# Where the weight splits, token sums and modulation sums of a trunk's first mixer run

## The chip, the cores and the metric

The kernel runs on one core of one Trainium2 chip. The metric is the device time of one execution in microseconds (us). A core has a matrix engine (PE, whose weight loads are shown as PEld), a vector engine (DVE), an activation engine (ACT), a general engine (POOL) and an engine that here only issues transfers (SP). Each takes its instructions in order; semaphores tie them together.

## The reference

Two layers of a trunk over 512 tokens of width 1024, all in float32. Every half layer is a sandwich with a modulation that comes from one vector c:

```python
def sandwich(x, mod, g_pre, g_post, fn):
    shift, scale, gate = mod
    h = rms_norm(x, g_pre) * (1.0 + scale[:, None]) + shift[:, None]
    return x + gate[:, None] * rms_norm(fn(h), g_post)
```

`mod` is `silu(c) @ w + b`, split in three. The first `fn` is the mixer that the change touches. It projects h to u, q, f, v and g. u goes through a pool mixer: for four groups of 128 features, a mean over the last 2, 4, 8 or 16 tokens less u, times a small matrix and a scale. q, f, v and g go through HGRN with 4 heads: with f' = lb + (1 - lb) sigmoid(f) as decay and k = (1 - lb) sigmoid(-f) as key, o[t] = q[t] applied to the decayed sum of k[s] v[s] over s <= t; then an RMS norm, a gain and silu(g). Both results are concatenated and projected (w_ho). The other three `fn` are a SwiGLU, a dilated attention and a SwiGLU.

## The kernel before, in words

**Layout.** h lies with features on the 128 partitions, 8 tiles of 512 tokens (k = 0 to 7). Every float32 product is made of three matmuls: an operand is split into a rounded part `hi` and the rest `lo = x - hi`, and hi*hi, lo*hi and hi*lo are added in a PSUM bank. A weight block is 128x1024 (512 KB). `load_next` (transfer L326, on SP) brings the next block, `split_next` makes `hi` by ACT (L351) and `lo` by `sub` (L284). `sub` puts every `by`-th subtraction on POOL, all on DVE when `by` is 0; for weights `by` is `share[0]`, which is 1 from the start (all on POOL), 2 from the gate on and 3 behind the mixer.

**Modulation.** 96 rows of the modulation's matrix, each 128x1025, are loaded into three buffers (`ada_load`, L390) and multiplied with silu(c) and summed by one DVE operation (`ada_half`, L403). Two halves are a step (`ada_step`): 0 to 7 give shift and scale of the first sandwich's eight tiles, 8 to 11 its gate, 12 to 19 shift and scale of the second. A small operation (L412, for all eight of a later sandwich L417) makes `s1 = (1 + scale) * gain`. The load of half i takes the buffer of half i - 3. `ADA` caps the steps in three stages of the mixer: 12 while the values are made, 20 in the pool stage, 20 in the gate's.

**First projections (to L550).** x is squared by ACT (L487) and added by DVE; PE sums over the partitions, DVE and POOL (a power, L475) make 1/rms, and PE spreads it over a bank (`rb_bank`). Then the loop over k, with the order of PE, ACT, DVE and SP written by hand (`hold` to `release`): DVE has `xr = x * rows` (L512, L538); ACT makes h_hi from it (L522, scale and shift as operands); DVE makes h again (`t`, L536) and h_lo = t - h_hi (L539). Block k of w_qf is split one round ahead, two halves of modulation for k + 1 are made, and 24 matmuls (L263) go into eight banks: q and f of four heads.

**The mixer (L880 to L1180).** Here a planner in the build orders the instructions of each engine by its own costs. ACT makes silu(q) and two sigmoids of f (L905, L906), DVE scales them (L908, L909). Twelve `level`s (128 small matmuls, L929, taken out by DVE, L930) and twelve `grow`s (DVE, L940, L941, L943) make the heads' products inside a 64-token tile; between them PE makes the values (w_v, 96 matmuls). The pool stage takes w_u block by block: ACT copies u (L1041), POOL makes the token sums by doubling (L1047, ten operations of 128x512), DVE finishes (L1053 to L1056), a split and three matmuls follow. Then come the cross blocks (L1081, L1091), copied by DVE (L1084, L1092), the gate (w_g, 96 matmuls) and the four heads (L1126 to L1164), among whose matmuls the first part of w_ho's lies.

**Later stages** are not touched: the second half of w_ho, SwiGLU, attention and SwiGLU, whose orders are written by hand with fixed places for splits (`ENDS`).

Of the kernel before, what the change touches and what calls it, by code (L numbers as in the profile page):

```python
# [12 lines left out]
F32 = mybir.dt.float32  # L13
# [7 lines left out]
ND = D // P  # L21
# [33 lines left out]
LAST_WARM = 3, 5  # L55
ADA = 12, 20, 20
G_SHARE = 2
EARLY = 3
# [122 lines left out]
def trunk(ctx: ExitStack, tc: tile.TileContext, a: dict, out: bass.AP, last: int = 3):  # L181
# [95 lines left out]
    turn = [0]  # L277
    share = [1]

# [115 lines left out]
    def ada_half(k):  # L395
        s, j = divmod(ada["at"], 12)
        i = 2 * ada["at"] + k
        if i < ada["next"]:
            return
        ada_load(i)  # L400
        w = ada["loaded"].pop(i)
        ada["next"] = i + 1
        dve.scalar_tensor_tensor(w, w, 1.0, sil, ALU.mult, ALU.mult, accum_out=mods[:, s, 2 * j + k : 2 * j + k + 1])  # L403

    def ada_step(until):
        if ada["at"] >= min(until, 48):
            return
        s, j = divmod(ada["at"], 12)
        for k in range(2):
            ada_half(k)  # L410
        if j < 8 and s == 0:
            dve.scalar_tensor_tensor(  # L412
                s1[:, s, j : j + 1], mods[:, s, 2 * j : 2 * j + 1], 1.0, npre[:, s, j : j + 1], ALU.add, ALU.mult
            )
        elif j == 7:
# [52 lines left out]
    tr.free(c_r)  # L468

    def rstd(sums, n, cols):  # L470

        v = col(cols)
        dve.tensor_scalar(v, sums, 1.0 / n, EPS, ALU.mult, ALU.add)  # L473
        r = col(cols)
        pool.tensor_tensor(r, v, mhalf[:, 0:cols], ALU.pow)  # L475
        return r
# [23 lines left out]
    tr.free(acc)  # L500
    ada_half(0)
    r = rstd(bk[b][:, 0:4], D, 4)
    ada_step(1)
    bk.free(b)
    weights(w_qf)
    keep_warm(WARM[1])
    rb_bank = bk.get()
    spread(rb_bank, r, 4)
    rb_r = tr.get(1)
    xr_rs = [tr.get(1) for _ in range(2)]  # L510
    xr = [tr.ap(z) for z in xr_rs]
    dve.tensor_tensor(xr[0], xT[:, 0, :], bk[rb_bank], ALU.mult)  # L512
    keep_warm(WARM[2])
# [4 lines left out]
    for k in range(ND):  # L518
        ada_load(2 * k + 2)
        ada_step(k + 1)  # L520
        ada_load(2 * k + 3)
        act.activation(h_hi[:, k, :], xr[k % 2], AF.Identity, bias=shift(0, k), scale=s1[:, 0, k : k + 1])  # L522
        if k == 0:
            act.activation(tr.ap(rb_r), bk[rb_bank], AF.Copy)
            bk.free(rb_bank)
            banks8.append(bk.get())
        hi, lo = weights(w_qf + k)
        for _ in range(1 + k % 2):
            load_next()
        if state["split"] <= w_qf + k + 1 < w_v:  # L530
            split_next()
        if k == 6:
            sp.dma_start(ar.ap(masks_r), a["masks"])
        t_r = tr.get(1)
        t = tr.ap(t_r)
        dve.tensor_scalar(t, xr[k % 2], s1[:, 0, k : k + 1], shift(0, k), ALU.mult, ALU.add)  # L536
        if k + 1 < ND:
            dve.tensor_tensor(xr[(k + 1) % 2], xT[:, k + 1, :], tr.ap(rb_r), ALU.mult)  # L538
        dve.tensor_tensor(h_lo[:, k, :], t, h_hi[:, k, :].bitcast(F32), ALU.subtract)  # L539
        tr.free(t_r)  # L540
        passes = ((hi, h_hi), (lo, h_hi), (hi, h_lo))
# [4 lines left out]
        weights_done(w_qf + k)  # L546
    for z in (rb_r, *xr_rs):
        tr.free(z)
# [353 lines left out]
    for h in range(4):  # L902
# [134 lines left out]
    for g in range(4):  # L1037
# [38 lines left out]
    for pr in range(2):  # L1076
# [5 lines left out]
        for i in range(2):  # L1082
            ps = slice(64 * i, 64 * i + 32)
            dve.tensor_copy(A[pr][ps, :, 64 * i + 32 : 64 * i + 64], bk[b][ps, 0:256].rearrange("p (n t) -> p n t", n=8))  # L1084
        bk.free(b)
        grow(pr, 32)
    for pr in range(2):
        b = bk.get()
        for n in range(8):
            o = n * P  # L1090
            pe.matmul(bk[b][0:64, n * 64 : n * 64 + 64], KS[pr][:, o : o + 64], QP[pr][:, o + 64 : o + 128], start=True, stop=True, skip_group_check=True)  # L1091
        dve.tensor_copy(A[pr][0:64, :, 64:128], bk[b][0:64, :].rearrange("p (n t) -> p n t", n=8))  # L1092
        bk.free(b)
# [9 lines left out]
    ahead.update(load=9, split=4, f=4)  # L1103
    share[0] = G_SHARE
    for h in range(4):
# [476 lines left out]
```

## Time and profile before

| | us |
|---|---|
| median of 3 runs | 1296.45 (1294.95 to 1298.38) |
| the profiled execution, in all | 1293.51 |
| its span, first to last instruction | 1291.70 |
| loop over k, first to last matmul | 17.63 to 72.34 |
| values to gate | 72.34 to 185.17 |
| heads and the first part of w_ho | 185.17 to 217.41 |

A line of the timeline gives start, duration, engine, line of the source, operation, output <- inputs, shape and count, and in brackets how long the engine had been idle and which work ended that. The granted clock (PEclk) is the share of full speed that PE was given; 0.985 over the execution. Grouped lines give the count, the busy time and the mean of one in ns.

### The profile page before, as it was taken

The page shows a single profiled execution, that of the slowest core. Times are in us where ns is not written, and L with a number is a line of the kernel's source. Part 1 is how long each engine was busy: PE and PEld are TensorE (multiplying, and loading weights), DVE is VectorE, ACT ScalarE, POOL GpSimd, SP SyncE. Part 2 cuts the span into 40 slices and gives each one's busy share as a digit, 9 for nine tenths or more (in the row PEclk, how much of TensorE's full clock was granted, in tenths as well). Part 3 has the DMA queues.
Part 4 walks back from the last instruction along what each step waited for, and adds up shares of the span by engine and source line. Part 5 has one row for each costly group of instructions (what it writes and reads, how often), then busy time and mean ns, then how long its engine had stood idle before and what let it go on. Part 6 is the DMA issues. An engine that isn't in the chain of part 4 may idle for free.

```text
span 1291.7 us, 20674 instructions
## 1 busy us (share of the span) xinstructions
PE 1236.8 (96%) x8672; PEld 1093.5 (85%) x8672; DVE 646.6 (50%) x965; ACT 453.5 (35%) x743; POOL 271.3 (21%) x141
## 2 busy tenths in 40 slices
PE   7897798999999999999999999999899999999997
PEld 5675588998888889999989978778898888889997
DVE  7997975766444222345767324336864111213415
ACT  4241434543222222224544324335742222222313
POOL 4641531312111102131311111011411111121002
PEclk9998899999999999999999999999999999999999
DMA  8855344144554223242348412124416222223301
GB/s 289 309 165 193 114 164 147 38 143 179 196 196 147 82 82 98 98 147 66 115 129 289 170 59 71 36 98 148 144 63 235 82 82 82 65 93 95 108 1 66
DMA packets 50383, 164.25 MB, mean 127 GB/s; under 512 B 5809, under 2 KB 11081, under 8 KB 50290
## 3 DMA queue, kind: packets, MB, share of 16 engines
q1 hardware_dynamic: 50290, 162.93, 37.2%
q8 instruction: 68, 1.11, 0.4%
q14 instruction: 25, 0.20, 0.0%
HBM read 160.78 MB, written 2.13 MB: 126 GB/s over the span
## 4 chain that ended last, share of the span: by engine, by line
PE 81%; DVE 12%; ACT 3%; issue 2%; POOL 1%; DMA 1%; SPq 0%; DVEq 0%; ACTq 0%; POOLq 0%
PE bank L263 78%; DVE ada_w L403 4%; PE bank L1374 1%; DVE t L642 1%; PE bank L1343 1%; DVE swing L941 1%; DVE swing L284 1%; DVE f L646 1%; DVE swing L940 1%; POOL cst L475 1%; DVE h L681 0%; DVE t L603 0%; DVE r L284 0%; POOL h L284 0%; DMA f<-x 0%
## 5 line engine op out<-in xcount | busy, mean ns | idle before, releaser
L263 PE MATMUL bank<-h,r 128*128 128x512 f32 (+1 forms) x2104 | 467.8, 364 | 15.5 <-DVE f L930 8.0
L263 PEld LDWEIGHTS bank<-h,r 128*128 128x128 f32 x2104 | 364.9, 192 | 78.5 <-ACT h L522 9.0
L263 PE MATMUL bank<-h,swing 128*128 128x512 f32 (+1 forms) x1664 | 325.1, 343 | 3.6 <-ACT swing L351 2.2
L263 PEld LDWEIGHTS bank<-h,swing 128*128 128x128 f32 x1664 | 268.5, 191 | 39.9 <-ACT swing L351 2.4
L284 POOL TENSOR_TENSOR r<-f,r 128x1024 fp32r<-128x1024 f32 x39 | 100.2, 2570 | 391.1 <-PE bank L263 289.0
L351 ACT ACTIVATE r<-f 128x1024 fp32r<-128x1024 f32 x104 | 109.1, 1057 | 134.5 <-PE bank L263 105.5
L263 PE MATMUL bank<-o,swing 128*128 128x256 f32 x1280 | 153.7, 276 | 0.0
L403 DVE SCALAR_TENSOR_TENSOR ada_w<-ada_w,sil 128x1025 f32<-128x1025 f32 x96 | 143.7, 1513 | 11.8 <-DMA ada_w<-ada 11.7
L263 PEld LDWEIGHTS bank<-o,swing 128*128 128x128 f32 x1280 | 149.1, 188 | 0.1
L284 DVE TENSOR_TENSOR r<-f,r 128x1024 fp32r<-128x1024 f32 (+1 forms) x51 | 65.1, 1277 | 167.3 <-PE bank L263 110.5
L284 POOL TENSOR_TENSOR swing<-f,swing 128x1024 fp32r<-128x1024 f32 x27 | 66.5, 2462 | 255.7 <-PE bank L263 209.0
L284 DVE TENSOR_TENSOR swing<-f,swing 128x1024 fp32r<-128x1024 f32 x45 | 59.9, 1335 | 119.9 <-PE bank L263 80.9
L351 ACT ACTIVATE swing<-f 128x1024 fp32r<-128x1024 f32 x80 | 83.5, 1058 | 85.9 <-PE bank L263 42.2
L263 PE MATMUL bank<-o,r 128*128 128x256 f32 x832 | 101.7, 275 | 0.0
L263 PEld LDWEIGHTS bank<-o,r 128*128 128x128 f32 x832 | 97.8, 188 | 0.1
L1196 ACT ACTIVATE t<-bank 128x512 f32<-128x512 f32 (+1 forms) x52 | 27.2, 531 | 175.3 <-PE bank L263 175.3
L263 PE MATMUL bank<-h,o 128*128 128x512 f32 (+1 forms) x312 | 80.8, 345 | 2.5 <-DVE h L681 1.7
L263 PE MATMUL bank<-r,h 128*128 128x512 f32 x288 | 71.9, 397 | 0.0
L263 PEld LDWEIGHTS bank<-r,h 128*128 128x128 f32 x288 | 61.7, 249 | 6.3 <-issue 0.4
L263 PEld LDWEIGHTS bank<-h,o 128*128 128x128 f32 x312 | 55.0, 188 | 11.1 <-DVE h L681 2.1
L475 POOL TENSOR_TENSOR cst<-cst 128x2 f32<-128x2 f32 (+1 forms) x19 | 17.9, 940 | 210.2 <-DVE cst L473 210.2
L284 DVE TENSOR_TENSOR o<-f,o 128x256 fp32r<-128x256 f32 (+2 forms) x37 | 24.8, 687 | 74.1 <-ACT o L565 70.3
(187 smaller groups left out, 1046.9 us busy)
## 6 DMA issues: line engine op xcount, KB each, us to landing
ada_w<-ada SPq DMA_DIRECT2D x96, 512.5 KB, 4.9
f<-w_fi SPq DMA_DIRECT2D x88, 512.0 KB, 4.8
f<-w_fo SPq DMA_DIRECT2D x44, 512.0 KB, 3.5
f<-w_aqk SPq DMA_DIRECT2D x24, 512.0 KB, 3.8
f<-w_av SPq DMA_DIRECT2D x12, 512.0 KB, 4.4
f<-w_qf SPq DMA_DIRECT2D x8, 512.0 KB, 4.7
f<-w_ho SPq DMA_DIRECT2D x8, 512.0 KB, 3.5
f<-x SPq DMA_DIRECT2D x8, 256.0 KB, 3.1
```

What stands on the lines that cost most here:

```text
L263: i = pe.matmul(o, lhsT, rhs, start=start, stop=stop, skip_group_check=True)
L284: eng.tensor_tensor(o, x, y, ALU.subtract)
L351: act.activation(hi, w, AF.Copy)
L403: dve.scalar_tensor_tensor(w, w, 1.0, sil, ALU.mult, ALU.mult, accum_out=mods[:, s, 2 * j + k : 2 * j + k + 1])
L475: pool.tensor_tensor(r, v, mhalf[:, 0:cols], ALU.pow)
L642: dve.tensor_tensor(us[i], us[i], rows, ALU.mult)
L646: (pool if i < 2 else dve).tensor_tensor(x, x, us[i], ALU.add)
L940: dve.tensor_tensor(qv, qv, t_first.unsqueeze(2).broadcast_to([P, n, L]), ALU.mult)
L941: dve.tensor_tensor(kv, kv, t_second.unsqueeze(2).broadcast_to([P, n, L]), ALU.mult)
L1196: act.activation(tr.ap(sa)[:, cols], a, AF.Silu)
L1343: pe.matmul(o, qc, kc, start=True, stop=True, skip_group_check=True)
L1374: pe.transpose(bk[b][:, seg * P : (seg + 1) * P], sc[:, i * P : (i + 1) * P], ident)
```

## The change

- All weight splits of the mixer's weights go to DVE: `share[0]` is 0 until the end of the mixer.
- h takes two DVE operations per tile: `u = x * s1 * rows`, then ACT makes h_hi = u + shift, and DVE h_lo = (u + shift) - h_hi.
- At the start two more transfers are issued ahead (modulation half 2, weight block 1). The second half of step 0 waits for POOL's power, and `s1` of a tile is made by `scale_of` as soon as its scale is there. In the loop the two halves stand on either side of h_lo; block 0 is split in the loop and no longer before it.
- The scalings of f' and k (L908, L909) and the copies of the cross blocks (L1084, L1092) go from DVE to ACT.
- The token sums (L1047) go from POOL to DVE.
- `ADA` is 9, 12, 16: one step with the values, three in the pool stage, four with the gate, and the last four with the heads, where `ada_step(20)` stood already.

```diff
-ADA = 12, 20, 20
-G_SHARE = 2
+ADA = 9, 12, 16
-    share = [1]
+    share = [0]
+    def scale_of(k):
+        dve.scalar_tensor_tensor(s1[:, 0, k : k + 1], mods[:, 0, 2 * k : 2 * k + 1], 1.0, npre[:, 0, k : k + 1], ALU.add, ALU.mult)
...
     load_next()
+    ada_load(2)
+    load_next()
...
     ada_half(0)
+    ada_load(3)
+    scale_of(0)
     r = rstd(bk[b][:, 0:4], D, 4)
-    ada_step(1)
+    tc.add_manual_dep(ada_half(1).ins, newest_rstd[0], SYNC, reason="they would slow each other down")
+    ada_load(4)
     bk.free(b)
-    weights(w_qf)
...
-    dve.tensor_tensor(xr[0], xT[:, 0, :], bk[rb_bank], ALU.mult)
...
     for k in range(ND):
-        ada_load(2 * k + 2)
-        ada_step(k + 1)
-        ada_load(2 * k + 3)
-        act.activation(h_hi[:, k, :], xr[k % 2], AF.Identity, bias=shift(0, k), scale=s1[:, 0, k : k + 1])
+        u = tr.ap(us_rs[k % 2])
+        rows = tr.ap(rb_r) if k else bk[rb_bank]
+        dve.scalar_tensor_tensor(u, xT[:, k, :], s1[:, 0, k : k + 1], rows, ALU.mult, ALU.mult)
+        hi, lo = weights(w_qf + k)
+        act.activation(h_hi[:, k, :], u, AF.Identity, bias=shift(0, k))
...
-        hi, lo = weights(w_qf + k)
+        ada["at"] = k + 1
+        if k + 1 < ND:
+            ada_half(0)
+            ada_load(2 * k + 5)
         for _ in range(1 + k % 2):
             load_next()
-        if state["split"] <= w_qf + k + 1 < w_v:
+        dve.scalar_tensor_tensor(h_lo[:, k, :], u, shift(0, k), h_hi[:, k, :].bitcast(F32), ALU.add, ALU.subtract)
+        if k + 1 < ND:
+            ada_half(1)
+            ada_load(2 * k + 6)
+            scale_of(k + 1)
             split_next()
...
-        dve.tensor_scalar(t, xr[k % 2], s1[:, 0, k : k + 1], shift(0, k), ALU.mult, ALU.add)
-        if k + 1 < ND:
-            dve.tensor_tensor(xr[(k + 1) % 2], xT[:, k + 1, :], tr.ap(rb_r), ALU.mult)
-        dve.tensor_tensor(h_lo[:, k, :], t, h_hi[:, k, :].bitcast(F32), ALU.subtract)
...
-        dve.tensor_scalar(FT[h // 2][:, sl], FT[h // 2][:, sl], lb1[:, h : h + 1], lb[:, h : h + 1], ALU.mult, ALU.add)
-        dve.tensor_scalar(KS[h // 2][:, sl], KS[h // 2][:, sl], lb1[:, h : h + 1], None, ALU.mult)
+        act.activation(FT[h // 2][:, sl], FT[h // 2][:, sl], AF.Identity, bias=lb[:, h : h + 1], scale=lb1[:, h : h + 1])
+        act.activation(KS[h // 2][:, sl], KS[h // 2][:, sl], AF.Copy, scale=lb1[:, h : h + 1])
...
-            pool.tensor_tensor(nxt[:, PADW:], cur[:, PADW:], cur[:, PADW - n : U_w - n], ALU.add)
+            dve.tensor_tensor(nxt[:, PADW:], cur[:, PADW:], cur[:, PADW - n : U_w - n], ALU.add)
...
-            dve.tensor_copy(A[pr][ps, :, 64 * i + 32 : 64 * i + 64], ...)
+            act.activation(A[pr][ps, :, 64 * i + 32 : 64 * i + 64], ..., AF.Copy)
...
-        dve.tensor_copy(A[pr][0:64, :, 64:128], ...)
+        act.activation(A[pr][0:64, :, 64:128], ..., AF.Copy)
...
-    share[0] = G_SHARE
```

More of the change, by code (lines that the diff above doesn't have):

```diff
@@ L258, in release @@
         held[0].__exit__(None, None, None)
+    SYNC = mybir.DependencyInfo(mybir.DependencyClass.Sync, mybir.DependencyReason.DATA)
     NOSYNC = mybir.DependencyInfo(mybir.DependencyClass.NoSync, mybir.DependencyReason.DATA)
@@ L402, in ada_half @@
         ada["next"] = i + 1
-        dve.scalar_tensor_tensor(w, w, 1.0, sil, ALU.mult, ALU.mult, accum_out=mods[:, s, 2 * j + k : 2 * j + k + 1])
+        return dve.scalar_tensor_tensor(w, w, 1.0, sil, ALU.mult, ALU.mult, accum_out=mods[:, s, 2 * j + k : 2 * j + k + 1])
     def ada_step(until):
@@ L410, in ada_step @@
             ada_half(k)
[L411 to L415, printed above, removed]
+        if j == 7:
             sc = mods[:, s, 0:16].rearrange("p (k two) -> p k two", two=2)[:, :, 0]
@@ L468, in trunk @@
     tr.free(c_r)
+    newest_rstd = [None]
     def rstd(sums, n, cols):
@@ L474, in rstd @@
         r = col(cols)
-        pool.tensor_tensor(r, v, mhalf[:, 0:cols], ALU.pow)
+        newest_rstd[0] = pool.tensor_tensor(r, v, mhalf[:, 0:cols], ALU.pow).ins.name
         return r
@@ L509, in trunk @@
     rb_r = tr.get(1)
-    xr_rs = [tr.get(1) for _ in range(2)]
-    xr = [tr.ap(z) for z in xr_rs]
-    dve.tensor_tensor(xr[0], xT[:, 0, :], bk[rb_bank], ALU.mult)
+    us_rs = [tr.get(1) for _ in range(2)]
     keep_warm(WARM[2])
@@ L533, in trunk @@
             sp.dma_start(ar.ap(masks_r), a["masks"])
-        t_r = tr.get(1)
-        t = tr.ap(t_r)
-        dve.tensor_scalar(t, xr[k % 2], s1[:, 0, k : k + 1], shift(0, k), ALU.mult, ALU.add)
-        if k + 1 < ND:
-            dve.tensor_tensor(xr[(k + 1) % 2], xT[:, k + 1, :], tr.ap(rb_r), ALU.mult)
-        dve.tensor_tensor(h_lo[:, k, :], t, h_hi[:, k, :].bitcast(F32), ALU.subtract)
-        tr.free(t_r)
         passes = ((hi, h_hi), (lo, h_hi), (hi, h_lo))
@@ L546, in trunk @@
         weights_done(w_qf + k)
-    for z in (rb_r, *xr_rs):
+    for z in (rb_r, *us_rs):
         tr.free(z)
@@ L1083, in trunk @@
             ps = slice(64 * i, 64 * i + 32)
-            dve.tensor_copy(A[pr][ps, :, 64 * i + 32 : 64 * i + 64], bk[b][ps, 0:256].rearrange("p (n t) -> p n t", n=8))
+            act.activation(A[pr][ps, :, 64 * i + 32 : 64 * i + 64], bk[b][ps, 0:256].rearrange("p (n t) -> p n t", n=8), AF.Copy)
         bk.free(b)
@@ L1091, in trunk @@
             pe.matmul(bk[b][0:64, n * 64 : n * 64 + 64], KS[pr][:, o : o + 64], QP[pr][:, o + 64 : o + 128], start=True, stop=True, skip_group_check=True)
-        dve.tensor_copy(A[pr][0:64, :, 64:128], bk[b][0:64, :].rearrange("p (n t) -> p n t", n=8))
+        act.activation(A[pr][0:64, :, 64:128], bk[b][0:64, :].rearrange("p (n t) -> p n t", n=8), AF.Copy)
         bk.free(b)
```

## The prediction

> **What bounds the kernel now.** I read the page's head first: it says which engine fills the span.
>
> ```profile
> span 1291.7 us, 20674 instructions
> PE 1236.8 (96%) x8672; PEld 1093.5 (85%) x8672; DVE 646.6 (50%) x965; ACT 453.5 (35%) x743; POOL 271.3 (21%) x141
> ```
>
> PE is busy for 96%, so only time in which PE waits, or runs at a lower granted clock, can be won. The change touches nothing behind the mixer; I cut what lies before that into stages by the windows view (us, then busy us of PE, PEld, DVE, ACT, POOL, then PEclk, DMA share, GB/s).
>
> ```profile
> 17.63:72.34 54.71, 47.80 (x193) 36.60 (x194) 53.89 (x67) 21.13 (x26) 29.93 (x10) 0.97 0.79 275
> 72.34:99.99 27.65, 27.65 (x473) 21.57 (x476) 26.01 (x42) 11.58 (x19) 10.69 (x5) 1.00 0.56 191
> 185.17:217.41 32.24, 27.45 (x216) 26.47 (x214) 18.12 (x30) 11.98 (x37) 6.52 (x5) 0.95 0.31 98
> 72.34:185.17 112.83, 97.62 (x1211) 76.11 (x1211) 98.27 (x149) 38.82 (x68) 42.72 (x23) 0.89 0.49 165
> ```
>
> The first row is the loop over the eight first weight blocks, the second the values' stage, the third the four heads, and the last the whole middle (values, levels, token sums, gate). In the loop DVE has 53.89 of 54.71 us: DVE is the bound there, not PE. In the middle PE lacks 112.83 - 97.62 = 15.2 us. The timeline of one loop block shows why DVE is full:
>
> ```profile
> 25.64 1.22 DVE L403 SCALAR_TENSOR_TENSOR ada_w<-ada_w,sil 128x1025 f32<-128x1025 f32 x1
> 26.79 0.08 DVE L403 DVE_READ_ACCUMULATOR ada_w<-ada_w,sil 128x1 f32 x1
> 26.79 3.41 DVE L403 SCALAR_TENSOR_TENSOR ada_w<-ada_w,sil 128x1025 f32<-128x1025 f32 x1
> 30.12 0.08 DVE L403 DVE_READ_ACCUMULATOR ada_w<-ada_w,sil 128x1 f32 x1
> 30.12 0.15 DVE L412 SCALAR_TENSOR_TENSOR cst<-cst 128x1 f32<-128x1 f32 x1
> 30.31 0.55 DVE L536 TENSOR_SCALAR t<-t,cst 128x512 f32<-128x512 f32 x1
> 30.77 0.69 DVE L538 TENSOR_TENSOR t<-f,t 128x512 f32<-128x512 f32 x1
> 31.37 0.69 DVE L539 TENSOR_TENSOR h<-t,h 128x512 fp32r<-128x512 f32 x1
> 31.98 1.22 DVE L403 SCALAR_TENSOR_TENSOR ada_w<-ada_w,sil 128x1025 f32<-128x1025 f32 x1
> ```
>
> ```profile
> 26.68 2.43 POOL L284 TENSOR_TENSOR r<-f,r 128x1024 fp32r<-128x1024 f32 x1 [3.90 <-ACT r L351]
> ```
>
> ```profile
> 30.31 0.81 ACT L522 ACTIVATE h<-t,cst 128x512 fp32r<-128x512 f32 x1 [3.71 <-DVE cst L412]
> ```
>
> ```profile
> 31.18 5.73 PE L263 MATMUL bank<-h,r 128*128 128x512 f32 x24 [0.60 <-ACT h L522]
> ```
>
> The same half of a modulation sum takes 1.22 us at 25.64 and 3.41 us at 26.79. In the second, POOL's weight split runs from 26.68 to 29.11; the half ends 1.1 us later. The two do not share: the half does its own work after POOL's. So one block costs DVE 31.98 - 25.64 = 6.34 us, of which 2.2 are waiting for POOL, while PE needs 5.73.
>
> **Start and loop.** The first block waits for a chain that has POOL in it:
>
> ```profile
> 12.86 1.94 POOL L475 TENSOR_TENSOR cst<-cst 128x4 f32<-128x4 f32 x1 [9.47 <-DVE cst L473]
> ```
>
> ```profile
> 206.76 1.01 POOL L475 TENSOR_TENSOR cst<-cst 128x4 f32<-128x4 f32 x1 [4.52 <-DVE cst L473]
> ```
>
> ```profile
> 14.85 1.16 PE L263 MATMUL bank<-cst 128*128 128x128 f32 x8 [1.22 <-POOL cst L475]
> ```
>
> The power at 12.86 took 1.94 us beside a half on DVE, the one at 206.76 1.01 without one. The change makes that half wait for it: the half, 1.2 us long, runs beside the 1.16 us of matmuls that spread the power's result. Queued behind it on DVE is the first operation for h, and PE waits for that. I take 0.8 us earlier (bounds 0 and 0.93, the power's whole excess). The small scale operation put ahead costs 0.15 of it (its row above).
>
> New DVE work per block: two halves at 1.15 (from 25.64 to the next start at 26.79), two operations for h at 0.60 (30.77 to 31.37) instead of three, the scale at 0.19, and the split that POOL did. Its price on DVE, and a run of PE without waits:
>
> ```profile
> 172.94 1.22 DVE L284 TENSOR_TENSOR r<-f,r 128x1024 fp32r<-128x1024 f32 x1
> ```
>
> ```profile
> 90.60 8.46 PE L263 MATMUL bank<-r,h 128*128 128x512 f32 x36
> ```
>
> 2 x 1.15 + 2 x 0.60 + 0.19 + 1.22 = 4.9 us. PE: 8.46 / 36 = 0.235 us, times 24 = 5.64. Loads: two halves of modulation and on average 1.5 weight blocks, all about 0.5 MB, the same as before. At 275 GB/s they hold 0.79 of the queues in 6.34 us a block, so 5.0 us when full. In SP's queue two more loads now lead, and from there each half's load waits for a half on DVE with a weight load behind it, as before. So PE becomes the bound, by 0.6 us over the loads and 0.7 over DVE. Loop end before and PE's first start:
>
> ```profile
> 17.63 5.87 PE L263 MATMUL bank<-h,o 128*128 128x512 f32 x24
> ```
>
> ```profile
> 65.03 7.31 PE L263 MATMUL bank<-h,r 128*128 128x512 f32 x24 [2.76 <-ACT h L522]
> ```
>
> Before, the loop runs from 17.63 to 65.03 + 7.31 = 72.34. After: 17.63 - 0.8 + 0.4 (the first block has two splits on DVE, so h of the second is late once) + 8 x 5.64 = 62.3. **Gain 10.0 us**, with the 1.6 us that the last block lost to its clock in it (7.31 against 5.73). Bounds: 5 us if blocks come at 6.34 again and only the start's 0.8, the last wait's 2.76 and its clock go; 10.8 at 5.56 a block (PE's 5.73 less the 0.17 in which its last matmul drains).
>
> **Middle.** What PE waits for there, and what its clock then costs:
>
> ```profile
> PE bank L263 <- DVE f L930: 8.0, 2, 6.3
> PE bank L1091 <- DVE swing L941: 2.3, 1, 2.3
> PE bank L1126 <- ACT swing L1109: 1.2, 1, 1.2
> PE bank L263 <- DVE r L284: 1.2, 1, 1.2
> ```
>
> ```profile
> 106.61 7.11 PE L263 MATMUL bank<-h,r 128*128 128x512 f32 x24 [6.30 <-DVE f L930]
> ...
> 147.41 6.75 PE L263 MATMUL bank<-h,r 128*128 128x512 f32 x22
> ...
> 162.81 7.29 PE L263 MATMUL bank<-h,r 128*128 128x512 f32 x21
> ```
>
> At 0.235 these are 5.64, 5.17 and 4.94: the clock after the waits cost 1.5 + 1.6 + 2.4 = 5.5 us. With the 15.2 of waiting, 20.7 us can be won. 11.5 of the 15.2 wait for DVE by the three rows. Why DVE is late:
>
> ```profile
> 104.97 1.23 DVE L403 SCALAR_TENSOR_TENSOR ada_w<-ada_w,sil 128x1025 f32<-128x1025 f32 x1 [2.44 <-DMA ada_w<-ada]
> ```
>
> ```profile
> L941 DVE TENSOR_TENSOR swing<-swing,swing 128x512 f32<-128x512 f32 x14 | 15.6, 1111 | 0.0
> ```
>
> The 6.3 us wait ends behind a half that itself waited 2.44 for its load; 8 halves lie among the values, of which 2 remain. L941 takes 1.11 on average where such an operation alone takes 0.69 (30.77): POOL again, whose ten token sums and weight splits all lie here.
>
> DVE's new load: it loses 8 of 24 halves (8 x 1.15 = 9.2 us), 8 scalings (8 x 0.55 = 4.4, by L536) and six small copies (3 by the same row, rather less). It gains ten token sums at 0.69 and some 12 splits at 1.22: 21.5. And it loses the waiting for POOL. Each of POOL's 23 operations in the middle can cost DVE 2.2 us, as in the loop, or nothing, when it falls into a gap: 0 to 50, though L941 alone shows 14 x 0.42 = 5.9. I take half, 25. 98.3 - 9.2 - 4.4 - 3 + 21.5 - 25 = 78; at the least saving 97. PE's own work is 97.62 - 5.5 = 92. So DVE falls from above PE to below it, but not by so much that no chain will wait. I take three quarters of the 11.5 (8.6) and, with those gaps gone, 4.4 of the 5.5: **gain 13 us** (bounds 3.9, the load's 2.44 and the clock's 1.5 behind it, and 20.7; nearer the upper, since the largest wait hangs on halves that leave).
>
> [...]
>
> To ACT go the eight scalings, at up to 0.81 (L522) 6.5 us, and the copies. ACT has 11.58 of 27.65 in the values' stage; what hides the scalings are the values' 96 matmuls, 22.6 us; without that cover they cost 6.5.
>
> **Heads.** Four steps (8 halves, 8 loads) come here: 9.2 us on DVE, which idles 32.24 - 18.12 = 14.1. The loads go into SP's queue ahead of loads for the next stage, which is far away. PE's 4.8 us of waiting here may grow: **loss 1 us** (bounds 0 and 5).
>
> **Sum.** 10 + 13 - 1 = 22 us. The profiled execution took 1293.51 in all, 1.8 more than its span, so 1271.5 for such a one; the median of the three runs is 1296.45, 2.9 above it. I forecast 1296.45 - 22 = 1274.5.
>
> **Rivals.** (a) DVE stays the middle's bound: if POOL cost it only the 5.9, it has 97 us to PE's 92. Then only the lower 3.9 us are won: 1296.45 - 10 - 4 + 1 = 1283.5. For it: DVE does every split. Against: the loop shows 2.2 us lost to each POOL operation.
> (b) All PE waits of the middle go: 10 + 20.7 with the heads hidden, 1266. For it: 11.5 of 15.2 hang on DVE. Against: some wait for ACT.
> (c) ACT decides the first level: the scalings stand ahead of it on ACT and PE runs dry, 6.5 lost: 1281. For it: 0.81 on ACT against 0.55 on DVE. Against: 22.6 us of cover. [...]
> (d) Slower: in the heads DVE stops for the moved sums' loads, in order, with the head's own operations behind them.
>
> ```profile
> ada_w<-ada SPq DMA_DIRECT2D x96, 512.5 KB, 4.9
> ```
>
> Two halves and one such landing per head, 2 x 1.15 + 4.9 = 7.2, times four 28.8: 1296.45 - 23 + 28.8 = 1302. It decides when a head's loads leave only after the head before has freed their buffers. For it: the 2.44 wait at 104.97. Against: queues are 0.31 busy there.
> (e) No change: the loop's gain comes back because the middle waits for the same loads or for an order of PE that no longer fits: 1296. Against: 0.49 of the queues.
>
> **Chances.** Forecast 0.55, (a) 0.20, (b) 0.12, (c) 0.06, (d) 0.04, (e) 0.03. A measurement tells 0.3% (3.9 us) from no change, so faster 0.93, same 0.03, slower 0.04. The range goes from (b) with all of the heads' waits won too, less 4: 1262, to (a) with 3 more lost in the heads: 1286.
>
> **What would show it.** Right: PE's loop starts come 5.6 apart, no half takes 3.4 beside POOL, the loop ends near 62, the last w_g matmul group and the heads lie some 23 us earlier, the 24 matmuls of 106.61 take 5.7 us wherever they land. Wrong: loop blocks at 6 or more with waits for loads; PE waiting for L930 or L941 as long as before; DVE waiting for ada_w loads in the heads; any difference behind the mixer.

## The result and the profile after

The changed kernel takes 1276.34 us (median of 4 runs, 1270.55 to 1279.24) against 1296.45 before: a ratio of 0.9836, with a 95% interval of 0.9813 to 0.9859. That is 20.1 us less, or 1.6%; the forecast was 22.

The profiled execution of the changed kernel took 1279.24 us, the slowest of its four; the profiled one before took 1293.51, below its median. So the two profiles lie only 14.3 us apart, less than the medians. The forecast's 22 lies inside the interval (18.3 to 24.2 us). The page's head of the changed kernel:

```profile
span 1277.4 us, 20640 instructions
PE 1236.7 (97%) x8672; PEld 1097.0 (86%) x8672; DVE 622.3 (49%) x974; ACT 461.4 (36%) x757; POOL 194.6 (15%) x110
```

POOL has 77 us less to do than before, and yet DVE has 24 us less too, though it took over more work (splits, token sums) than it gave to ACT: before, much of what was booked as DVE's time was standing still (in a loop block 2.2 of 6.34 us). The windows view of the changed kernel (us; busy us of PE, PEld, DVE, ACT, POOL; PEclk, DMA share, GB/s):

```profile
20.59:65.82 45.23, 44.74 (x195) 35.76 (x193) 42.11 (x72) 20.45 (x25) 0.00 (x0) 1.00 0.90 326
121.67:149.00 27.33, 21.96 (x156) 15.96 (x156) 23.37 (x41) 13.55 (x20) 0.00 (x0) 0.88 0.44 153
167.00:201.58 34.58, 28.03 (x197) 27.07 (x197) 20.95 (x37) 12.72 (x43) 6.51 (x5) 0.80 0.32 106
65.82:167.00 101.18, 95.10 (x1229) 75.12 (x1229) 81.10 (x144) 46.07 (x75) 0.37 (x3) 0.97 0.51 180
```

The first row is the loop: PE is busy for 44.74 of 45.23 us, DVE for 42.11. The bound has changed from DVE to PE. The last row is the middle: PE lacks 6.1 us, where it lacked 15.2, and 5.4 of them lie in the second row, the pool stage with the cross blocks, where the clock is 0.88 as well. The third row, the heads, has a clock of 0.80; it was 0.95.

One loop block on DVE in the timeline of the changed kernel:

```profile
25.16 1.22 DVE L403 SCALAR_TENSOR_TENSOR ada_w<-ada_w,sil 128x1025 f32<-128x1025 f32 x1
...
26.31 0.75 DVE L538 SCALAR_TENSOR_TENSOR h<-t,cst,h 128x512 fp32r<-128x512 f32 x1
26.97 1.23 DVE L403 SCALAR_TENSOR_TENSOR ada_w<-ada_w,sil 128x1025 f32<-128x1025 f32 x1
...
28.12 0.16 DVE L420 SCALAR_TENSOR_TENSOR cst<-cst 128x1 f32<-128x1 f32 x1
28.19 1.22 DVE L284 TENSOR_TENSOR r<-f,r 128x1024 fp32r<-128x1024 f32 x1
29.32 0.75 DVE L525 SCALAR_TENSOR_TENSOR t<-f,cst,t 128x512 f32<-128x512 f32 x1
29.99 1.23 DVE L403 SCALAR_TENSOR_TENSOR ada_w<-ada_w,sil 128x1025 f32<-128x1025 f32 x1
```

From 25.16 to 29.99 it is 4.83 us (6.34 before), with the split inside, and neither half is longer than 1.23. PE's rows of the loop:

```profile
20.59 5.84 PE L263 MATMUL bank<-h,o 128*128 128x512 f32 x24
26.28 11.05 PE L263 MATMUL bank<-h,r 128*128 128x512 f32 x48
37.82 7.56 PE L263 MATMUL bank<-h,r 128*128 128x512 f32 x32 [0.49 <-ACT h L527]
...
54.50 11.32 PE L263 MATMUL bank<-h,r 128*128 128x512 f32 x48
```

Two blocks take 11.05 to 11.32, and one wait of 0.49 is left. To compare stages I cut each profile at the same four events: PE's first loop matmul, the loop's end, the matmuls that turn the first head's result back (L1161 before, L1165 after), and the start of the long run of 302 matmuls behind the mixer.

| | time | ratio to before | first matmul | loop | middle | heads |
|---|---|---|---|---|---|---|
| before | 1296.45 | 1 | 17.63 | 54.71 | 117.50 | 27.57 |
| changed | 1276.34 | 0.9836 | 20.59 | 45.24 | 106.65 | 29.10 |
| changed, again | 1275.62 | 0.9824 | 19.93 | 44.66 | 105.40 | 27.98 |
| splits on POOL | 1283.48 | 0.9899 | 18.18 | 52.56 | 110.83 | 29.81 |
| token sums on POOL | 1278.02 | 0.9836 | 18.76 | 44.62 | 105.98 | 29.49 |
| modulation as before | 1284.06 | 0.9882 | 19.79 | 45.97 | 112.02 | 27.62 |
| splits alone | 1292.89 | 0.9972 | 20.01 | 61.01 | 105.36 | 28.42 |
| scalings, copies on DVE | 1282.90 | 0.9892 | 18.44 | 44.99 | 112.98 | 27.54 |
| POOL reads | 1286.59 | 0.9923 | 18.63 | 56.13 | 105.19 | 29.13 |
| POOL fills | 1275.98 | 0.9841 | 16.94 | 46.87 | 107.19 | 28.97 |
| splits alone, behind | 1281.17 | 0.9885 | 19.88 | 50.39 | 103.26 | 27.63 |
| sums with values | 1276.94 | 0.9848 | 18.74 | 44.95 | 107.30 | 26.77 |
| sums later | 1280.32 | 0.9878 | 18.30 | 45.02 | 104.94 | 34.13 |
| scalings alone on DVE | 1277.96 | 0.9858 | 19.69 | 45.24 | 106.90 | 29.03 |

The stages are of one profile each, times and ratios of all runs, against the kernel before on the same chip. Between the two profiles: first matmul 3.0 us later, loop 9.5 shorter, middle 10.8 shorter, heads 1.5 longer, and the untouched rest 1.5 longer: together 14.3 us less. That rest (span less the start of the 302 matmuls) takes 1074.3 us before, 1075.8 after, and 1074.5 to 1077.7 in the twelve profiles of the experiments, so no effect can be seen in it.

### The profile page after: what moved, and what is told of

Same layout as the page of the kernel before. It is cut to its first block, busy times and chain, and to the rows that moved or that the text cites. A ratio compares the mean times of both kernels' runs of the same rounds, so it can differ in the third digit from the quotient of the medians.

```text
span 1277.4 us, 20640 instructions
## 1 busy us (share of the span) xinstructions
PE 1236.7 (97%) x8672; PEld 1097.0 (86%) x8672; DVE 622.3 (49%) x974; ACT 461.4 (36%) x757; POOL 194.6 (15%) x110
## 4 chain that ended last, share of the span: by engine, by line
PE 86%; DVE 7%; ACT 2%; issue 2%; DMA 1%; POOL 1%; SPq 0%; DVEq 0%; ACTq 0%; POOLq 0%
PE bank L263 83%; PE bank L1378 1%; DVE t L647 1%; PE bank L1347 1%; DVE ada_w L403 1%; DVE r L284 1%; DVE swing L284 1%; DVE f L651 1%; DMA f<-w_qf 1%; DMA ada_w<-ada 0%; DVE h L686 0%; DVE t L608 0%; PE bank L934 0%; POOL h L284 0%; DMA f<-x 0%
## 5 line engine op out<-in xcount | busy, mean ns | idle before, releaser
L263 PE MATMUL bank<-h,r 128*128 128x512 f32 (+1 forms) x2104 | 460.1, 360 | 3.7 <-DVE r L284 2.0
L263 PEld LDWEIGHTS bank<-h,r 128*128 128x128 f32 x2104 | 360.4, 189 | 64.9 <-DVE r L284 3.2
L284 DVE TENSOR_TENSOR r<-f,r 128x1024 fp32r<-128x1024 f32 x64 | 80.1, 1252 | 169.6 <-PE bank L263 94.3
L403 DVE SCALAR_TENSOR_TENSOR ada_w<-ada_w,sil 128x1025 f32<-128x1025 f32 x96 | 125.1, 1317 | 12.4 <-DMA ada_w<-ada 11.3
L284 POOL TENSOR_TENSOR r<-f,r 128x1024 fp32r<-128x1024 f32 x26 | 63.2, 2432 | 353.2 <-PE bank L263 240.8
L263 PEld LDWEIGHTS bank<-h,o 128*128 128x128 f32 x312 | 55.1, 188 | 10.1 <-DVE h L686 2.1
```

The source lines that it names most:

```text
L263: i = pe.matmul(o, lhsT, rhs, start=start, stop=stop, skip_group_check=True)
L284: eng.tensor_tensor(o, x, y, ALU.subtract)
L403: return dve.scalar_tensor_tensor(w, w, 1.0, sil, ALU.mult, ALU.mult, accum_out=mods[:, s, 2 * j + k : 2 * j + k + 1])
```

## The experiments

The theory: a POOL operation that reads keeps DVE out for its whole length. The change takes such operations out of the loop and the middle, and PE then is the bound in the loop. The rivals: it is only the amount and the order of work on DVE that count; or the parts that went to ACT and to later stages bring the gain.

### The changed kernel again

> The changed kernel once more, unedited. Its first profile showed the loop's first matmul at 20.59 us, 3 us later than before the change, where the prediction had 16.8, because the token tiles of x arrived late (sums done at 12.5) and PE then ran at half clock until 20. If that is chance of one execution, this profile shows the first matmul at 16.8 to 18 and a time near 1270 to 1274. If it belongs to the change (the extra transfers ahead, the wait for the power), it shows 20 to 21 again and 1275 to 1279.

It took 1275.62 us (1270.43 to 1280.44, 6 runs), ratio 0.9824 (0.9799 to 0.9850): the same. The first loop matmul came at 19.93, late again and between the alternatives; the time is that of the second, by which the late start belongs to the change. Against this speak the profiles of all runs together, as the account of the start below shows. The loop took 44.66.

### The splits back on POOL

```diff
-    share = [0]
+    share = [1]
...
     ahead.update(load=9, split=4, f=4)
+    share[0] = 2
```

> The changed kernel with the weight splits as before (all on POOL up to the gate, every second one from there). Exclusion theory (a POOL operation that reads SBUF and a DVE operation with two SBUF inputs shut each other out): a loop block costs DVE 4.83 - 1.14 + 2.2 to 2.4, so 5.9 to 6.1 against PE's 5.65; loop 2 to 4 us longer, middle 3 to 5 longer, time 5 to 9 above the changed kernel. Work theory (the loop is shorter because DVE has fewer and better placed operations of its own): DVE is relieved of 20 splits, loop stays at 45.2, time the same or up to 3 lower.

1283.48 us (1281.39 to 1292.19), ratio 0.9899 (0.9869 to 0.9929): 7.9 us above the changed kernel on the same chip, as the theory had it. The profiled execution took 1290.56, 7 above that median. Rows of POOL, DVE and PE in this kernel's loop:

```profile
25.73 3.41 POOL L284 TENSOR_TENSOR r<-f,r 128x1024 fp32r<-128x1024 f32 x1 [2.66 <-ACT r L351]
```

```profile
25.67 1.22 DVE L403 SCALAR_TENSOR_TENSOR ada_w<-ada_w,sil 128x1025 f32<-128x1025 f32 x1
...
26.81 2.35 DVE L420 SCALAR_TENSOR_TENSOR cst<-cst 128x1 f32<-128x1 f32 x1
29.19 0.75 DVE L525 SCALAR_TENSOR_TENSOR t<-f,cst,t 128x512 f32<-128x512 f32 x1
```

```profile
30.76 5.75 PE L263 MATMUL bank<-h,r 128*128 128x512 f32 x24 [0.28 <-ACT h L527]
```

Read the middle one: an operation on one element per partition takes 2.35 us, where it takes 0.16 in the changed kernel. It stands still until POOL's split has ended at 29.14. POOL in turn took 3.41 instead of 2.43, since DVE's half was running when it came. In these rows the two take turns, by whole instructions. Blocks come 6.0 apart (24.75, 30.76, 36.76), as expected. The loop as a whole was put 2 to 4 us longer and is 7.3 longer in this profile, since PE waits another 2.25 and 0.75 us ahead of the last two blocks.

### The token sums back on POOL

```diff
-            dve.tensor_tensor(nxt[:, PADW:], cur[:, PADW:], cur[:, PADW - n : U_w - n], ALU.add)
+            pool.tensor_tensor(nxt[:, PADW:], cur[:, PADW:], cur[:, PADW - n : U_w - n], ALU.add)
```

> The changed kernel with the ten token sums on POOL again. Exclusion theory: each shuts DVE out for some 1.4 us in place of 0.6 of DVE's own, 0 to 8 us of DVE in the pool stage, time 1 to 5 above the changed kernel. Work theory: DVE is relieved of 6 us in its fullest stage, time the same or up to 3 lower.

1278.02 us (1273.78 to 1279.61), ratio 0.9836 (0.9815 to 0.9856): inside the first expectation (1 to 5 above), but its interval overlaps that of the unedited kernel, so no effect of this part is shown.

### The modulation sums as before

```diff
-ADA = 9, 12, 16
+ADA = 12, 20, 20
```

> The changed kernel with the modulation caps of before (12, 20, 20): eight halves go back among the values and none lies in the heads. By the prediction's steps the wait for DVE behind the values comes back in part (0 to 8 us) and the heads win 1 to 2.4: time 0 to 6 above the changed kernel. Rival: without POOL in its way DVE has room for the halves among the values, and only the heads' gain is left: 1 to 2.4 below.

1284.06 us (1278.31 to 1286.22), ratio 0.9882 (0.9861 to 0.9904): 8.4 us slower, more than the 0 to 6 that I expected. The middle is 112.02 us, 5.4 longer than in the changed kernel's first profile and 6.6 than in the second, and PE waits for the levels again:

```profile
PE bank L263 <- DVE f L935: 2.8, 2, 1.8
```

### Only the splits, in the kernel before

```diff
-    share = [1]
+    share = [0]
...
-    share[0] = G_SHARE
```

> The kernel before with one edit of the change alone: every weight split on DVE, none on POOL; the power, the half beside it, the three operations for h, the scalings, the copies, the token sums and the modulation sums stay as they were. If POOL keeps DVE out for the length of a split (in the kernel before a half took 3.41 us, not 1.22, beside one): the old loop block of DVE is 6.34 - 2.2 + 1.14 = 5.3 us, PE's 5.65 takes over, so loop starts 5.6 to 5.75 apart and a loop of 45 to 47 us (54.7 before); in the middle the splits leave POOL too, and PE's waits there shrink by several us; in all 12 to 16 us below the kernel before, and the rest of the changed kernel's gain is from its other parts. If instead it is the amount of DVE's work that counts: the block gets no shorter than 6, and the time is at most 4 us below the kernel before. It also tells about the start, which it leaves as it was: PE's first loop matmul at 17 to 18.5 us and the eight sums in 1.05 us if the late start (19.9 to 20.6 in two profiles of the changed kernel) belongs to the change, 19.5 or later if it comes and goes by itself.

1292.89 us (1291.99 to 1293.77), ratio 0.9972 (0.9959 to 0.9985): only 3.2 us, not 12 to 16. By the number the rival has it, yet the stages say otherwise. The middle became as short as the changed kernel's (105.36), and the loop **longer** than before, 61.01. The halves are all at 1.22 now; but ACT and DVE in one block:

```profile
36.55 0.81 ACT L522 ACTIVATE h<-t,cst 128x512 fp32r<-128x512 f32 x1 [5.31 <-DVE cst L412]
37.27 1.04 ACT L351 ACTIVATE r<-f 128x1024 fp32r<-128x1024 f32 x1
```

```profile
36.37 0.15 DVE L412 SCALAR_TENSOR_TENSOR cst<-cst 128x1 f32<-128x1 f32 x1
38.34 1.23 DVE L284 TENSOR_TENSOR r<-f,r 128x1024 fp32r<-128x1024 f32 x1 [1.83 <-ACT r L351]
39.49 0.54 DVE L536 TENSOR_SCALAR t<-t,cst 128x512 f32<-128x512 f32 x1
```

DVE makes the scale at 36.37; ACT makes h with it and then the rounded weights; and DVE's next instruction is the split, which needs those. DVE stands for 1.83 us, with the operations for h queued behind it. POOL, whose queue held nothing else, could wait there for free (3.90 us at 26.68 in the kernel before). The block is 5.24 of work and 1.83 of waiting: 7.07.

### The scalings and copies back on DVE

```diff
-        act.activation(FT[h // 2][:, sl], FT[h // 2][:, sl], AF.Identity, bias=lb[:, h : h + 1], scale=lb1[:, h : h + 1])
-        act.activation(KS[h // 2][:, sl], KS[h // 2][:, sl], AF.Copy, scale=lb1[:, h : h + 1])
+        dve.tensor_scalar(FT[h // 2][:, sl], FT[h // 2][:, sl], lb1[:, h : h + 1], lb[:, h : h + 1], ALU.mult, ALU.add)
+        dve.tensor_scalar(KS[h // 2][:, sl], KS[h // 2][:, sl], lb1[:, h : h + 1], None, ALU.mult)
...
-            act.activation(A[pr][ps, ...], bk[b][ps, 0:256]..., AF.Copy)
+            dve.tensor_copy(A[pr][ps, ...], bk[b][ps, 0:256]...)
...
-        act.activation(A[pr][0:64, :, 64:128], bk[b][0:64, :]..., AF.Copy)
+        dve.tensor_copy(A[pr][0:64, :, 64:128], bk[b][0:64, :]...)
```

> The changed kernel with the eight scalings of f' and k and the six copies of the cross blocks back on DVE. By the prediction's step (96 matmuls cover them on either engine): the changed kernel's time to within 2 us. [...] If DVE still is what PE waits for among the values and levels: slower by 1 to 4 us.

1282.90 us (1281.23 to 1283.27), ratio 0.9892 (0.9876 to 0.9908): 7 us slower than the changed kernel by the ratios (0.0056 of 1296), beyond the expectations. The pool stage of this kernel in the windows view, and PE's longest wait in it:

```profile
119.30:146.60 27.30, 19.44 (x141) 14.39 (x141) 24.07 (x43) 10.64 (x13) 0.00 (x0) 0.81 0.37 121
```

```profile
138.16 0.49 PE L263 MATMUL bank<-o 128*128 128x512 f32 x1 [3.98 <-ACT o L570]
```

PE is busy for 19.44 of 27.3 us (21.96 in the changed kernel), at a clock of 0.81. Followed back, this wait is not one for a DVE that is full:

```profile
136.13 1.23 DVE L403 SCALAR_TENSOR_TENSOR ada_w<-ada_w,sil 128x1025 f32<-128x1025 f32 x1 [2.70 <-DMA ada_w<-ada]
137.28 0.16 DVE L1061 TENSOR_TENSOR f<-f 128x8 f32<-128x8 f32 x1
137.47 0.63 ACT L570 ACTIVATE o<-f 128x512 fp32r<-128x512 f32 x1 [1.47 <-DVE f L1061]
```

ACT's operation waits for a small one of DVE (L1061), and that stands in DVE's queue behind a half, for whose load DVE idled 2.70 us. In the changed kernel the planner put the same small operation at 133.76, ahead of a half that starts at 137.64 after 1.77 us of waiting for its load.

### An operation of POOL that reads, and three that write

The two kernels add work to each loop block on POOL that nobody waits for, either

```diff
+        again = h_hi[:, k, :].bitcast(F32).unsqueeze(1).broadcast_to([P, 2, T])
+        pool.tensor_tensor(tr.ap(idle_r).rearrange("p (n t) -> p n t", n=2), again, again, ALU.add)
```

or

```diff
+        for _ in range(3):
+            fill = pool.memset(tr.ap(idle_r), 0.0)
+            tc.add_manual_dep(fill.ins, hh.ins.name, SYNC, reason="once a block")
```

> The changed kernel with one operation added to each of the eight loop blocks: on POOL, a sum of 128x1024 elements that are read twice from h and written to a buffer that nobody uses (some 2.4 us). No step of the computation waits for it. If POOL's reading keeps DVE out: a half or a split that falls beside it takes over 3 us, DVE's block is 4.8 + 2.3 = 7.1 us, loop starts come some 7 us apart, and the loop takes 9 to 12 us more than the changed kernel's 45. If what the change won in the loop is only that h and the weights no longer wait for POOL's results: no difference.

> The changed kernel with three fills of 128x1024 with zeros added on POOL to each of the eight loop blocks, into a buffer that nobody uses: about as long on POOL as the added sum of the other kernel, but nothing is read. [...]

With the reading sum: 1286.59 us (1281.21 to 1289.48), ratio 0.9923 (0.9903 to 0.9943), 11 us above the changed kernel, and the loop 56.13. With the fills: 1275.98 us (1273.33 to 1277.65), ratio 0.9841 (0.9822 to 0.9860), no difference, and the loop 46.87, 1.6 and 2.2 longer than in the changed kernel's two profiles; PE waits 1.6 us for h in two places there, but no DVE instruction of that loop takes more than 1.23. The loop's rows of both in the windows view, reads first:

```profile
18.63:74.76 56.13, 48.26 (x194) 36.37 (x192) 55.55 (x73) 20.48 (x26) 15.98 (x8) 0.97 0.79 278
```

```profile
16.94:63.81 46.87, 45.16 (x192) 35.71 (x192) 42.76 (x73) 20.84 (x26) 22.93 (x24) 1.00 0.91 326
```

With 15.98 us of reading on POOL DVE's instructions last 55.55 us, with 22.93 us of writing 42.76 (42.11 in the changed kernel, with neither). The rows behind it, first POOL and DVE where POOL reads:

```profile
26.38 1.99 POOL L530 TENSOR_TENSOR t<-h 128x1024 f32<-128x1024 f32 x1 [5.67 <-ACT h L528]
```

```profile
26.54 2.37 DVE L541 SCALAR_TENSOR_TENSOR h<-t,cst,h 128x512 fp32r<-128x512 f32 x1
```

and where POOL writes:

```profile
28.06 2.98 POOL L530 MEMSET t<- 128x1024 f32 x3 [2.11 <-ACT h L528]
```

```profile
28.25 0.75 DVE L542 SCALAR_TENSOR_TENSOR h<-t,cst,h 128x512 fp32r<-128x512 f32 x1
```

The second operation for h (L541 and L542 here), 0.75 us long, takes 2.37 beside the first and 0.75 beside the second. DVE's work is the same in both. So in these two kernels what counts is not that POOL is busy but that it reads. It was the operation for h that paid, not a half or a split as I had written, and blocks came 6.45 apart, not 7; the loop's 10.9 us are in the range.

What DVE reads counts too, by the next rows. Behind the mixer the changed kernel still has splits on POOL, and there two DVE instructions follow each other beside the same one:

```profile
303.07 2.40 POOL L284 TENSOR_TENSOR swing<-f,swing 128x1024 fp32r<-128x1024 f32 x1 [13.92 <-PE bank L263]
```

```profile
303.27 0.69 DVE L1201 TENSOR_TENSOR swing<-t,bank 128x512 f32<-128x512 f32 x1 [3.31 <-PE bank L263]
303.88 2.69 DVE L403 SCALAR_TENSOR_TENSOR ada_w<-ada_w,sil 128x1025 f32<-128x1025 f32 x1
```

The first, which reads one of its two operands from a PSUM bank, takes the 0.68 us that it takes alone; the half, which reads both from SBUF, takes 2.69 instead of 1.22. The same pair beside the splits at 335.71 and 368.35 takes 0.69, then 2.69 and 2.68. So the theory as I put it, that DVE is kept out, is too wide.

### The splits alone, behind the operations for h

On top of the run with the splits alone:

```diff
         for _ in range(1 + k % 2):
             load_next()
-        if state["split"] <= w_qf + k + 1 < w_v:
-            split_next()
...
         dve.tensor_tensor(h_lo[:, k, :], t, h_hi[:, k, :].bitcast(F32), ALU.subtract)
         tr.free(t_r)
+        if state["split"] <= w_qf + k + 1 < w_v:
+            split_next()
```

> The kernel of the run with the splits alone (1292.9 us), with one more edit: in the loop, DVE's split of the next weight block stands behind the operations for h, not ahead of them. In that run no half was longer than 1.23 us, and yet the loop took 61 us: DVE stopped at each split for ACT's rounded copy of the weights (1.83 us a block in the steady part: 0.72 for h, then 1.04 for the copy, both behind DVE's own scale), with h's operations queued behind it. If that order is what ate the gain: DVE's block falls from 7.07 to 5.3 us, PE's 5.65 is the bound, the loop takes 45 to 47 us, and the time is about 1278 to 1281, all but 2 to 5 us of the whole change's gain, since the middle of that run was already as short as the changed kernel's (133.8 us from loop end to the long run of matmuls, against 135.8). If the two loads that the change issues earlier are needed too: the loop stays above 50 us, with waits for w_qf, and the time above 1284.

1281.17 us (1280.37 to 1281.64), ratio 0.9885 (0.9869 to 0.9902): 11.7 us less than without this edit, which moves two lines. Two splits of this kernel on DVE, and PE in its loop:

```profile
34.50 1.23 DVE L284 TENSOR_TENSOR r<-f,r 128x1024 fp32r<-128x1024 f32 x1
...
39.93 1.23 DVE L284 TENSOR_TENSOR o<-f,r 128x1024 fp32r<-128x1024 f32 x1
```

```profile
33.58 14.61 PE L263 MATMUL bank<-h,r 128*128 128x512 f32 x56 [2.20 <-ACT h L522]
```

The split waits no more, and DVE's block is 5.43 us. The time is just above the first expectation (1278 to 1281), but the loop took 50.39, not 45 to 47, and so lies on the second one's side: three waits of PE (2.20, 0.94 and 0.30 us) stay. Ahead of the first, ACT had waited 3.01 us for a block of w_qf. So the split's place is most of what the bare splits lacked, and the rest of the loop's gain (5 us of loop) belongs to the change's other parts there: the loads issued ahead and the shorter h. These two were not told apart.

### Three steps of modulation elsewhere

```diff
-ADA = 9, 12, 16
+ADA = 12, 12, 16
```

> The changed kernel with three steps (6 halves, 6.9 us of DVE) of the modulation moved from the token sums' stage ahead to the values' stage (due steps 12, 12, 16 instead of 9, 12, 16). In the changed kernel's profile DVE is busy for 23.4 of 27.3 us from 121.67 to 149.00, where PE idles 5.4 us and its clock is 0.88, and for 19.9 of 28.9 among the values, where PE does not wait. If DVE's share of that later stage is what is left to win: 3 to 6 us faster than the changed kernel. If the halves among the values push back the levels that follow (in order on DVE): 0 to 4 us slower.

1276.94 us (1274.06 to 1277.99), ratio 0.9848 (0.9829 to 0.9867): no difference, so the first of the two expectations, 3 to 6 us won, fell; the second (0 to 4 us slower) holds. DVE's share of the pool stage is not, by itself, what is left there. And the other direction, `ADA = 9, 9, 16`:

> The changed kernel with the same three steps moved out of the token sums' stage in the other direction, past the gate, so that the heads and what follows them have seven steps and not four (due steps 9, 9, 16). If DVE's share of the token sums' stage is what is left: 3 to 6 us won there, and 0 to 6 lost behind it, since each half in the heads stands ahead of a head's own operations and four steps there cost about 1 to 2 us; in all -5 to +2. By the heads' rival of the prediction (DVE stops for the loads) it would be slower by 5 or more.

1280.32 us (1280.28 to 1280.38), ratio 0.9878 (0.9861 to 0.9894): 5 us slower by the ratios, outside the -5 to +2 of the first expectation and at the edge of the rival's. Against the changed kernel's first profile the middle is 1.7 us shorter and the heads are 5.0 longer, 34.13. PE waits there for the sums' queue:

```profile
PE bank L1165 <- DVE cst L413: 3.8, 1, 3.8
```

L413 is the operation for the next sandwich's scales, right behind a half. DVE itself waits 2.6 us in the heads for the loads of modulation, in four places; in the changed kernel it doesn't wait for them there. Three more steps cost the heads 1.7 us each; that the change's four are what the heads bear is a guess from this.

### The scalings alone on DVE

The first four lines of the diff of the scalings and copies, without the copies.

> The changed kernel with the eight scalings of f' and k back on DVE, and the six copies of the cross blocks left on ACT. With both back the kernel took 1282.9 us, some 7 more than the changed kernel, which neither the prediction's step (0) nor its bounds for a busy DVE (1 to 4) gave; in that profile the first level's copy came 11.5 us behind the loop's end, in the changed kernel 13.5, so the scalings themselves were not late on DVE. If the copies cost the 7 us (they stand in DVE's fullest stretch, 24.1 of 27.3 us): this kernel takes the changed kernel's time or up to 2 us less. If the scalings do: 1281 or more.

1277.96 us (1277.38 to 1279.61), ratio 0.9858 (0.9839 to 0.9877): 1.6 to 2.3 us above the changed kernel's two medians and not below, but not to be told from them. So of the 7 us some 4.4 ((0.9892 - 0.9858) x 1296) come with the six copies, though the two intervals just touch. With the copies on ACT the planner also has the small operation (L1061) at 132.24, ahead of the half that waits for its load (136.57). So the copies' price may be that order rather than DVE's time on them (six operations); no run tells the two apart. The first level taken out by DVE, here and in the changed kernel:

```profile
76.16 0.45 DVE L935 COPY_PREDICATED f<-f,bank 128x256 f32<-128x256 int32 x1 [1.22 <-PE bank L934]
```

```profile
79.35 0.44 DVE L935 COPY_PREDICATED f<-f,bank 128x256 f32<-128x256 int32 x1
```

From the loop's end (64.93 and 65.83) it is 11.2 us here and 13.5 with the scalings on ACT. So ACT does delay the first level, as the prediction's rival (c) has it, by 2.3 us; PE waits for it in neither kernel, since the values' matmuls cover it.

## Why the prediction was right, step by step

**Loop: right.** By its working the loop alone would be 0.4 + 8 x 5.64 = 45.5 us; it is 45.24 and 44.66. DVE's block was put at 4.9 and is 4.83, though the two operations for h cost 0.66 each from start to start, not 0.60; the late second h (0.4) is not seen. That POOL's reading makes DVE stand is shown by the added sum and the added fills (2.37 and 0.75 us for the same operation). What the prediction did not say: the splits' place in DVE's queue matters as much as the engine. With the splits moved and the order kept the loop got 6.3 us longer; with the change's order and the splits on POOL it is 2.1 shorter; with both 9.5.

**Start: the step held, and what it left out was larger.** 0.8 us were to come from POOL's power without a half beside it. The power did fall, from 1.94 to 1.02:

```profile
14.73 1.02 POOL L479 TENSOR_TENSOR cst<-cst 128x4 f32<-128x4 f32 x1 [11.35 <-DVE cst L477]
```

but PE began 3.0 later, not 0.8 earlier. PE's rows of the start, first one of the kernel before, then the changed kernel's:

```profile
11.35 1.05 PE L263 MATMUL bank<-cst,t 128*128 128x1 f32 x8 [0.34 <-DVE t L491]
```

```profile
12.59 1.87 PE L263 MATMUL bank<-cst,t 128*128 128x1 f32 x8 [1.28 <-DVE t L495]
14.32 2.48 PE L263 MATMUL bank<-f 128*128 128x128 f32 x10
16.59 1.91 PE L263 MATMUL bank<-cst 128*128 128x128 f32 x8
```

Two things are seen, and the prediction has neither. x arrived late, so that the sums over the partitions began at 12.59. And PE ran at about half its speed: the eight sums took 1.87, and the ten warm-up matmuls 2.48, where they took 1.36 before. They stand ahead of the spread in PE's queue and held it to 16.59, though the power had ended at 15.75.

The second is a matter of the clock. The windows view can't show it, for it counts the time ahead of a trace's first clock record as full clock. The records themselves, which say from when on which share of the clock was granted, can. In all fourteen traces they change the clock only at whole steps of 3.41 us, between half and full, and where the steps begin differs from profile to profile. In the profile before, its records lie 1 to 193 such steps apart. Ahead of the sums lie 18 warm-up matmuls, from about 7.0 to 11 us. In eight profiles these fill one step to 86% or more; the first record of full clock stands at its end, at 10.0 to 11.4 us (10.56 in the kernel before), and the sums take 1.05. In the other six they fill no step beyond 78%; the first record of full clock comes at 16.2 to 20.0 us (20.00 in the changed kernel's first profile), and the sums take 1.86 or 1.87. This sorts all fourteen, but it was found afterwards, and no run was made to test it. The change moves nothing in the warm-up, and one of the six has the old start (the splits alone).

In six of the eight the clock falls back for a step or two before the loop. Only two profiles keep it full up to the loop: the kernel before and the one with the fills, whose start is the changed kernel's.

```profile
11.64 1.05 PE L263 MATMUL bank<-cst,t 128*128 128x1 f32 x8 [0.33 <-DVE t L495]
```

```profile
16.94 5.87 PE L263 MATMUL bank<-h,o 128*128 128x512 f32 x24
```

From the sums to the first loop matmul it is 5.30 us there and 6.28 before (11.35 to 17.63). So at the same clock the step wins 1.0 us, by one profile each, and the first matmul comes at 16.94, where the prediction had 16.8. Over all profiles the clock hides that: with the old start the first matmul came at 17.63, 20.01 and 19.88, with the new one anywhere from 16.94 to 20.59 in eleven; the means are 19.2 and 18.9. Why x comes late stays open.

**Middle: right in size, not in its reasons.** Forecast 13; by the table 10.8 and, in the second profile, 12.1. Cut where the prediction cut (at the end of the last matmuls of L1126, L1130 after: 166.65 and 164.16), it is 12.0 and 13.3. The waits went as forecast, the clock did not give all of its part: PE's waiting fell by 9.1 and 10.1 us (forecast 8.6), its busy time by 2.9 and 3.1 (forecast 4.4). The named wait is gone: PE doesn't wait for the levels (L935) at all. What is left of waits, from the changed kernel's view of 10 to 220 us:

```profile
PE bank L1165 <- DVE t L1160: 3.3, 1, 3.3
PE bank L263 <- DVE r L284: 2.8, 3, 1.6
PE bank L263 <- ACT swing L351: 2.2, 1, 2.2
```

The longest wait of the second row (1.6) ends behind a split that stands in DVE's queue behind the half at 137.64.

DVE's load was estimated at 78 us and is 81.1. Two steps behind the 13 were choices without a row: half of the 50 us that POOL could cost DVE, and three quarters of the 11.5 us of waits. That the size came out is in part luck, for the reasons do not add up in that way. The prediction gave the gain to the halves that leave and to the freed levels together. The splits alone bring the whole of it: 12.1 us in the kernel with the splits alone and 14.2 in the one with the splits behind h, with the token sums on POOL, the scalings and copies on DVE and the modulation as it was. And with the splits on POOL the other moves bring 6.7 (117.50 less 110.83). So the parts don't add, and how the others pay is not shown: each was put back only in the changed kernel, where it costs 7 us (scalings and copies) or 8.4 (modulation), while the kernels with the splits alone do without them. The planner orders the middle anew in every kernel, and in the one case followed back (the scalings and copies) that order made the wait. The prediction let 96 matmuls hide the scalings, which holds (1.6 to 2.3 us, not to be told from nothing); it gave the copies no price on ACT.

**Clock in the middle.** 22 matmuls, 5.17 us by the prediction's 0.235 each, took 6.93 behind a gap of 1.60, with shorter gaps ahead of it:

```profile
142.41 6.93 PE L263 MATMUL bank<-h,r 128*128 128x512 f32 x22 [1.60 <-DVE r L284]
```

The longest of those gaps is 1.60. The granted clock over these 6.93 us was 0.75: half from 142.88 to 146.29, full after that. The 22 matmuls from 129.63, behind a gap of 0.42, took 5.29 at a clock of 1.00.

**Heads: right.** Loss 1; by the table 1.5 and 0.4, by the prediction's cut 2.7 and 1.6, within its bounds of 0 and 5. DVE did not wait for the moved sums' loads there (rival (d)); with three more steps it did, for 2.6 us, and the heads took 5 us longer.

**Rivals.** (a), DVE as the middle's bound, did not come in time; that pieces put back on DVE cost 7 and 8.4 us speaks for a part of it. (b) did not come, 6.1 us of waits are left. (c) holds in its delay and not in its price. (d) and (e) did not come.

**Sum.** 22, against 20.1 measured. Term by term, between the profile before and the two of the changed kernel: the start lost 3.0 and 2.3 us (forecast 0.8 won), the loop won 9.5 and 10.1 (forecast 9.2), the middle 10.8 and 12.1 (13), the heads lost 1.5 and 0.4 (1). The profile before had the full clock at its start and these two had not, so they understate the gain, and where the missing 1.9 us lie between the medians can't be told from them. The mechanism of the loop is shown; that of the middle is in part argued.

## What to carry to other kernels

Look for short DVE instructions that last as long as a POOL instruction beside them; in these runs, where POOL read and DVE read both operands from SBUF, POOL's work was not beside DVE's but in turn with it (a half of 1.22 us took 2.69 or 3.41), and DVE did the same split itself in 1.22 us, less than the 2.2 that the standing had cost it. When an operation goes to an engine whose queue runs in order, look at what it waits for and at what is queued behind it (DVE stood 1.83 us a block at a split that waited for ACT): the same split gained 3 us or 15, by its place. After such a move look at each further piece in the stage in which it lands, and at what now stands behind a half that waits for its load. And before a late start is blamed on a change, see in several profiles when the clock first became full (here at 10.0 to 11.4 us or at 16.2 to 20.0).

The shortest middle is that of the run with the splits behind h (103.26), the shortest loops are those of the kernels with the changed kernel's whole loop (44.6 to 46.0). A kernel with the change's start and loop and only the splits in the middle might be faster by another 2 to 3 us (106.65 or 105.40 less 103.26); it was not run, and the stages are not independent.

## What the runs showed of the hardware that was not expected

- A DVE instruction on 128x1 elements took 2.35 us beside a POOL split and 0.16 without, 2.19 more; the half of 1.22 that took 3.41 in the kernel before stood for 2.19 too. So in these two the standstill did not scale with DVE's own work. In the other direction POOL's split took 3.41 us, not 2.43, when a half was ahead of it.
- Three fills on POOL, 2.98 us, took nothing from DVE (0.75 us with and without).
- A DVE instruction of 128x512 with one operand from a PSUM bank took 0.69 us beside a POOL split, as alone (0.68); the half behind it, with both operands from SBUF, took 2.69, not 1.22.
- At the start the eight sums took 1.05 or 1.86 to 1.87 us from one profile to the next. The gaps of PE ahead of them do not sort them; the place of the clock's 3.41 us steps does, in all fourteen profiles: 1.05 where the warm-up matmuls filled one step to 86% or more, 1.86 where they filled none beyond 78%.
